# A strided row copy in HBM: half of the rows by way of SBUF, in two-batch transfers

## The chip, the core and the metric

The kernel runs on one core of a Trainium2 chip. Its time is device microseconds of one launch. No compute engine does any of the work: SyncE (SP) and ScalarE (ACT) only issue transfers, each on a hardware queue of its own, and the core's 16 DMA engines carry them out.

## What is computed

The reference takes every second row of the first 512 rows of each of 32 batches:

```python
batch, seq, dim = 32, 1024, 512
x = np.random.randn(batch, seq, dim).astype(np.float32)
start, stop, stride = 0, 512, 2
return x[:, start:stop:stride, :].astype(np.float32)
```

One row is 512 floats, 2 KB. The output has 32 x 256 = 8192 rows, 16.78 MB. In `x` a wanted row begins every 4 KB, and a batch every 2 MiB. In the output rows follow one another without a gap, and a batch begins every 512 KiB. Both tensors lie in HBM, so at least 16.78 MB are read there and 16.78 MB written.

## The kernel before

The file holds several ways to do this copy; the constant `STRATEGY` (line 10) picks `_d2d_2q` (line 43), and the other functions are never called. `_d2d_2q` issues one transfer for each batch, straight from `x` to the output within HBM, the even batches on SP and the odd ones on ACT (line 49). Each transfer is 256 rows, 512 KiB. Nothing is computed and no transfer depends on another.

Semaphores are put in by the tile framework. It uses eight in turn, four on each queue, so the fifth transfer of a queue is issued only after the first has landed. At the end SP waits for all of them (these waits carry line 241, where the framework's context closes).

Of the kernel before, what the change touches and what calls it, by code (L numbers as in the profile page):

```python
# [1 line left out]

# [4 lines left out]


STRATEGY = "d2d_2q"  # L10

SLAB_SHARES = (11, 11, 10)

D2D2_SHARES = (10, 10, 12)


def _d2d(tc, x, out, start, stop, stride):
    nc = tc.nc
    B = x.shape[0]
    src = x[:, start:stop:stride, :]  # L20
    engines = [nc.sync, nc.scalar, nc.gpsimd]
    chunks = [(b, min(b + 1, B)) for b in range(0, B, 1)]
    for i, (b0, b1) in enumerate(chunks):
        eng = engines[i % len(engines)]
        eng.dma_start(out[b0:b1], src[b0:b1])


def _d2d_slab(tc, x, out, start, stop, stride):
    nc = tc.nc
    B = x.shape[0]  # L30
    src = x[:, start:stop:stride, :]
    engines = [nc.sync, nc.scalar, nc.gpsimd]
    shares = SLAB_SHARES
    assert sum(shares) == B
    b0 = 0
    for eng, n in zip(engines, shares):
        if n <= 0:
            continue
        eng.dma_start(out[b0 : b0 + n], src[b0 : b0 + n])
        b0 += n  # L40


def _d2d_2q(tc, x, out, start, stop, stride):
    nc = tc.nc
    B = x.shape[0]
    src = x[:, start:stop:stride, :]
    engines = [nc.sync, nc.scalar]
    for b in range(B):
        engines[b % 2].dma_start(out[b : b + 1], src[b : b + 1])


def _d2d_2q_stagger(tc, x, out, start, stop, stride):
    nc = tc.nc
    B = x.shape[0]
    n_out = out.shape[1]
    half = n_out // 2
    src = x[:, start:stop:stride, :]

    def full(b):
        return (out[b : b + 1], src[b : b + 1])  # L60

    def halfc(b, h):
        r0 = h * half
        r1 = r0 + half
        return (out[b, r0:r1], src[b, r0:r1])

    sync_chunks = [full(b) for b in range(0, 30, 2)] + [halfc(30, 0), halfc(30, 1)]
    scalar_chunks = [halfc(1, 0)] + [full(b) for b in range(3, 32, 2)] + [halfc(1, 1)]
    assert len(sync_chunks) == len(scalar_chunks) == 17

    for (od, sd), (od2, sd2) in zip(sync_chunks, scalar_chunks):
        nc.sync.dma_start(od, sd)
        nc.scalar.dma_start(od2, sd2)


def _d2d_2q_faststart(tc, x, out, start, stop, stride):
    nc = tc.nc
    B = x.shape[0]
    n_out = out.shape[1]
    half = n_out // 2  # L80
    src = x[:, start:stop:stride, :]

    nc.gpsimd.dma_start(out[0, 0:half], src[0, 0:half])
    sync_chunks = [(out[0, half:n_out], src[0, half:n_out])] + [
        (out[b : b + 1], src[b : b + 1]) for b in range(2, 32, 2)
    ]
    scalar_chunks = [(out[b : b + 1], src[b : b + 1]) for b in range(1, 32, 2)]
    for i in range(max(len(sync_chunks), len(scalar_chunks))):
        if i < len(sync_chunks):
            nc.sync.dma_start(*sync_chunks[i])  # L90
        if i < len(scalar_chunks):
            nc.scalar.dma_start(*scalar_chunks[i])


def _d2d2(tc, x, out, start, stop, stride):
    nc = tc.nc
    B = x.shape[0]
    src = x[:, start:stop:stride, :]
    n_sync, n_scalar, n_pool = D2D2_SHARES
    assert n_sync + n_scalar + n_pool == B  # L100
    order = []
    order += [(nc.gpsimd, b) for b in range(n_sync + n_scalar, B)]
    for i in range(max(n_sync, n_scalar)):
        if i < n_sync:
            order.append((nc.sync, i))
        if i < n_scalar:
            order.append((nc.scalar, n_sync + i))
    for eng, b in order:
        eng.dma_start(out[b : b + 1], src[b : b + 1])


def _d2d3(tc, x, out, start, stop, stride, shares=(8, 8, 16)):
    nc = tc.nc
    B = x.shape[0]
    src = x[:, start:stop:stride, :]
    n_sync, n_scalar, n_pool = shares
    assert n_sync + n_scalar + n_pool == B
    seq = []
    iters = max(n_sync, n_scalar, max(1, n_pool // 2))
    bs = 0  # L120
    ba = n_sync
    bp = n_sync + n_scalar
    for i in range(iters):
        if i < n_sync:
            seq.append((nc.sync, bs + i))
        if i * 2 < n_pool:
            seq.append((nc.gpsimd, bp + 2 * i))
        if i < n_scalar:
            seq.append((nc.scalar, ba + i))
        if i * 2 + 1 < n_pool:  # L130
            seq.append((nc.gpsimd, bp + 2 * i + 1))
    assert len(seq) == B
    for eng, b in seq:
        eng.dma_start(out[b : b + 1], src[b : b + 1])


def _d2d_swdge(tc, x, out, start, stop, stride, nchunks=32):
    nc = tc.nc
    B = x.shape[0]
    src = x[:, start:stop:stride, :]  # L140
    step = B // nchunks
    for i in range(nchunks):
        b0 = i * step
        nc.gpsimd.dma_start(out[b0 : b0 + step], src[b0 : b0 + step])


def _d2d_hw2(tc, x, out, start, stop, stride, batches_per_chunk=2):
    nc = tc.nc
    B, S, D = x.shape
    n_out = out.shape[1]  # L150
    src = x[:, start:stop:stride, :]
    engines = [nc.sync, nc.scalar]
    bpc = batches_per_chunk
    chunks = [(b, min(b + bpc, B)) for b in range(0, B, bpc)]
    for i, (b0, b1) in enumerate(chunks):
        eng = engines[i % len(engines)]
        n = b1 - b0
        s_ap = src[b0:b1].transpose([1, 0, 2])
        d_ap = out[b0:b1].transpose([1, 0, 2])
        eng.dma_start(d_ap, s_ap)  # L160


def _sbuf_pipelined(ctx, tc, x, out, start, stop, stride):
    nc = tc.nc
    B, S, D = x.shape
    n_out = out.shape[1]
    q = 2
    P = 128
    assert n_out == q * P

    src = x[:, start:stop:stride, :]

    pool = ctx.enter_context(tc.tile_pool(name="io", bufs=6))
    for b in range(B):
        t = pool.tile([P, q * D], out.dtype, name="t")
        nc.sync.dma_start(t, src[b].rearrange("(p q) d -> p q d", q=q))
        nc.scalar.dma_start(out[b].rearrange("(p q) d -> p (q d)", q=q), t)


@with_exitstack  # L180
def kernel(
    ctx: ExitStack,
    tc: tile.TileContext,
    x: bass.AP,
    start: bass.AP,
    stop: bass.AP,
    stride: bass.AP,
    out: bass.AP,
):
    nc = tc.nc  # L190
    assert isinstance(start, int) and isinstance(stop, int) and isinstance(stride, int)

    if STRATEGY == "d2d":
        _d2d(tc, x, out, start, stop, stride)
    elif STRATEGY == "d2d_2q":
        _d2d_2q(tc, x, out, start, stop, stride)
    elif STRATEGY == "d2d_2q_stagger":
        _d2d_2q_stagger(tc, x, out, start, stop, stride)
    elif STRATEGY == "d2d_2q_faststart":
        _d2d_2q_faststart(tc, x, out, start, stop, stride)  # L200
    elif STRATEGY == "d2d_slab":
        _d2d_slab(tc, x, out, start, stop, stride)
    elif STRATEGY == "d2d2":
        _d2d2(tc, x, out, start, stop, stride)
    elif STRATEGY == "d2d3":
        _d2d3(tc, x, out, start, stop, stride)
    elif STRATEGY == "d2d_swdge":
        _d2d_swdge(tc, x, out, start, stop, stride)
    else:
        _sbuf_pipelined(ctx, tc, x, out, start, stop, stride)  # L210


# [1 line left out]
_INS = ['x', 'start', 'stop', 'stride']  # L214
_OUTS = [((32, 256, 512), 'float32')]
#: Inputs that are plain numbers.
_NUMBERS = {'start': 0, 'stop': 512, 'stride': 2}


# [26 lines left out]
```

## Time and profile before

| What | Value |
|---|---|
| time, median of 13 runs | 84.71 us (83.82 to 86.12) |
| the profiled execution's own time | 84.92 us |
| its span, first to last instruction | 83.1 us |
| transfers | 32 of 512 KiB |
| HBM traffic over the span | 404 GB/s, reads and writes together |

The span leaves out what a launch does around the first and last instruction; in the profiled execution that is 84.92 - 83.1 = 1.8 us. In the profile q1 and q10 are the two hardware queues. A packet is here one row of 2 KB, or a small one that raises a semaphore. The share of a queue is the time that its packets took, added up, as a share of 16 engines' span. GB/s counts each copied byte once, though a copy within HBM touches HBM twice. Instructions that issue transfers are not counted as busy, so a table of engines is nearly empty for this kernel.

### The profile page before, as it was taken

Reading aid. Unit: us, or ns where it says so; the run is one execution under the profiler, and the core shown is the slowest. Engines: PE = TensorE matmul, PEld = TensorE weight load, DVE = VectorE, ACT = ScalarE, POOL = GpSimd, SP = SyncE. Lnnn points to the kernel's source line nnn. Section 1 sums busy time; section 2 is a strip of 40 time slices with the busy share of each in tenths; the row PEclk is TensorE's granted clock in tenths of the full one; section 3 lists DMA queues with packets and bytes.
Section 4 is the critical chain, followed back from the end, with each engine's and each line's share of the span. In section 5 each row is a group of like instructions: output and inputs, shape, how many; then the busy total and the mean of one; then the engine's idle time right before and its main releaser. Section 6 shows DMA issues by size and latency. Waiting matters only on the chain. (4 is left out here: it accounts for less than half of the span.)

```text
span 83.1 us, 77 instructions
## 1 busy us (share of the span) xinstructions
POOL 0.2 (0%) x4
## 2 busy tenths in 40 slices
POOL 0000000000000000000000000000000000000000
DMA  0989998999999799999989989997888999998950
GB/s 0 215 217 133 270 214 171 260 198 208 197 227 228 189 200 255 220 211 222 192 203 232 209 154 251 234 225 211 172 272 198 194 229 235 215 241 200 195 164 14
DMA packets 8704, 16.78 MB, mean 202 GB/s; under 512 B 512, under 2 KB 512, under 8 KB 8704
## 3 DMA queue, kind: packets, MB, share of 16 engines
q1 hardware_dynamic: 4352, 8.39, 49.9%
q10 hardware_dynamic: 4352, 8.39, 39.2%
HBM read 16.78 MB, written 16.78 MB: 404 GB/s over the span
## 5 line engine op out<-in xcount | busy, mean ns | idle before, releaser
L227 POOL MEMSET const-bfloat16-1.0<- 128x1 bf16 x1 | 0.1, 101 | 0.0
L227 POOL MEMSET const-uint8-127<- 128x1 uint8 x1 | 0.1, 101 | 0.0
L227 POOL MEMSET const-float32-0.0<- 128x1 f32 x1 | 0.1, 98 | 0.2 <-issue 0.2
L227 POOL MEMSET const-float32-1.0<- 128x1 f32 x1 | 0.1, 98 | 0.0
## 6 DMA issues: line engine op xcount, KB each, us to landing
out_dram<-in_x_dram ACTq DMA_DIRECT2D x16, 512.0 KB, 19.3
out_dram<-in_x_dram SPq DMA_DIRECT2D x16, 512.0 KB, 19.5
```

What stands on the lines that cost most here:

```text
L227: nc = _bacc.Bacc("TRN2", target_bir_lowering=False, num_devices=1)
```

## The change

The new kernel splits the rows of each batch by the parity of their number in the output. One parity is copied directly within HBM, as before; the other is loaded into SBUF and stored from there. Which parity goes which way alternates with bit 1 of the batch number (`apart`).

Each transfer covers one parity of two batches, ordered row by row: row 0 of the first batch, row 0 of the second, row 2 of the first, and so on (`two`). That is again 256 rows of 2 KB.

The batches are treated in four groups of eight. The pairs differ by kind of transfer. Loads take neighbours (0 and 1, 2 and 3, ...). Direct copies take 0 and 5, 2 and 7, 1 and 4, 3 and 6. Stores take batches four apart (0 and 4, 1 and 5, ...).

SP issues all 16 loads, ACT all 16 direct copies. Then, group by group, both wait until the four loads of the group have landed, and the group's four stores are issued in turn on SP and ACT. One SBUF tile (`held`, 128 partitions x 32 x 512 floats) keeps the whole staged half, so no buffer is reused. Semaphores are placed by hand: one for each group's loads, and one for each queue's remaining transfers, on which SP waits at the end.

```diff
-STRATEGY = "d2d_2q"
+EIGHT = 8
+def apart(b):
+    return 1 - (b >> 1 & 1)
+def two(t, b, step, parity):
+    return t[b : b + step + 1 : step].rearrange("b (p two) d -> two p b d", two=2)[parity]
...
-def _d2d_2q(tc, x, out, start, stop, stride):
-    nc = tc.nc
-    B = x.shape[0]
-    src = x[:, start:stop:stride, :]
-    engines = [nc.sync, nc.scalar]
-    for b in range(B):
-        engines[b % 2].dma_start(out[b : b + 1], src[b : b + 1])
...
     src = x[:, start:stop:stride, :]
+    B, rows, D = out.shape
+    P = rows // 2
+    sp, act = nc.sync, nc.scalar
+    groups = range(0, B, EIGHT)
+    with tc.tile_pool(name="io", bufs=1) as io:
+        held = io.tile([P, B, D], x.dtype, name="held")
+        with tc.tile_critical():
+            loaded = [nc.alloc_semaphore(name=f"loaded{g}") for g in groups]
+            done = [nc.alloc_semaphore(name=f"done{i}") for i in range(2)]
+            for g in groups:
+                for i, (b, step) in enumerate(((0, 5), (2, 5), (1, 3), (3, 3))):
+                    b += g
+                    at = g + 2 * i
+                    sp.dma_start(held[:, at : at + 2], two(src, at, 1, 1 - apart(at))).then_inc(loaded[g // EIGHT], 16)
+                    act.dma_start(two(out, b, step, apart(b)), two(src, b, step, apart(b))).then_inc(done[1], 16)
+            for g in groups:
+                for queue in (sp, act):
+                    queue.wait_ge(loaded[g // EIGHT], 16 * 4)
+                for b in range(g, g + 4):
+                    k = b % 2
+                    to = two(out, b, 4, 1 - apart(b))
+                    (sp, act)[k].dma_start(to, held[:, b : b + 5 : 4]).then_inc(done[k], 16)
+            sp.wait_ge(done[0], 16 * (B // 4))
+            sp.wait_ge(done[1], 16 * (B // 2 + B // 4))
```

More of the change, by code (lines that the diff above doesn't have):

```diff
@@ L2 @@
-from contextlib import ExitStack
 import concourse.bass as bass
 import concourse.tile as tile
-from concourse import bass_utils, mybir
-from concourse._compat import with_exitstack
-STRATEGY = "d2d_2q"
-SLAB_SHARES = (11, 11, 10)
-D2D2_SHARES = (10, 10, 12)
-def _d2d(tc, x, out, start, stop, stride):
+from concourse import mybir
+EIGHT = 8
[3 more added lines that the diff above has]
+    return t[b : b + step + 1 : step].rearrange("b (p two) d -> two p b d", two=2)[parity]
@@ L18, in _d2d, with kernel @@
+def kernel(tc, x, start, stop, stride, out):
     nc = tc.nc
-    B = x.shape[0]
     src = x[:, start:stop:stride, :]
[L21 to L28, printed above, removed]
-    nc = tc.nc
-    B = x.shape[0]
-    src = x[:, start:stop:stride, :]
[L32 to L40, printed above, removed]
@@ L43, in _d2d_2q @@
-def _d2d_2q(tc, x, out, start, stop, stride):
-    nc = tc.nc
-    B = x.shape[0]
-    src = x[:, start:stop:stride, :]
-    engines = [nc.sync, nc.scalar]
-    for b in range(B):
[L49 to L73, printed above, removed]
@@ L76, in _d2d_2q_faststart @@
[L76 to L92, printed above, removed]
@@ L95, in _d2d2 @@
[L95 to L109, printed above, removed]
@@ L112, in _d2d3 @@
[L112 to L134, printed above, removed]
@@ L137, in _d2d_swdge @@
[L137 to L160, printed above, removed]
@@ L163, in _sbuf_pipelined @@
[L163 to L177, printed above, removed]
@@ L180 @@
[L180 to L210, printed above, removed]
+    B, rows, D = out.shape
```

## The prediction

> **What bounds the kernel now.** I read the page's head first, then the DMA rows, then the waits of SP's own queue, then the stretches of time. The head and the rows of the page:
>
> ```profile
> span 83.1 us, 77 instructions
> ...
> GB/s 0 215 217 133 270 214 171 260 198 208 197 227 228 189 200 255 220 211 222 192 203 232 209 154 251 234 225 211 172 272 198 194 229 235 215 241 200 195 164 14
> DMA packets 8704, 16.78 MB, mean 202 GB/s; under 512 B 512, under 2 KB 512, under 8 KB 8704
> ...
> q1 hardware_dynamic: 4352, 8.39, 49.9%
> q10 hardware_dynamic: 4352, 8.39, 39.2%
> HBM read 16.78 MB, written 16.78 MB: 404 GB/s over the span
> ...
> out_dram<-in_x_dram ACTq DMA_DIRECT2D x16, 512.0 KB, 19.3
> out_dram<-in_x_dram SPq DMA_DIRECT2D x16, 512.0 KB, 19.5
> ```
>
> No compute engine works; everything is 8192 packets of one 2 KB row each, plus 512 small ones that count semaphores. The two queues together hold the 16 DMA engines for 49.9 + 39.2 = 89.1% of the span, 74.0 us of 83.1. Divided among the rows that is 0.891 x 83.1 x 16 / 8192 = 145 ns for one row. The second row of numbers is rates in slices of 2.1 us: they swing from 133 to 272 about a mean near 214.
>
> ```profile
> SPq L49 <- DMA out_dram<-in_x_dram: 50.9, 12, 5.0
> ```
>
> SP's queue waits 50.9 us in all before it issues, but that starves nobody: a transfer lands 19.4 us after its issue, and eight transfers of 524,288 bytes at 214 GB/s take 19.6 us, so eight stand queued at all times. The stretches show the same:
>
> ```profile
> 0.00:2.00 2.00, 0.20 (x4) 1.00 0.00 0
> ...
> 40.00:48.00 8.00, 0.00 (x0) 1.00 0.97 215
> 48.00:56.00 8.00, 0.00 (x0) 1.00 0.98 215
> ...
> 78.00:80.00 2.00, 0.00 (x0) 1.00 0.93 214
> 80.00:81.00 1.00, 0.00 (x0) 1.00 0.29 96
> ```
>
> The last two columns are the engines' busy share and GB/s. From 2 to 80 us the engines are held 95% of the time at about 214 GB/s. So the kernel is 78.0 us of steady copying, and 84.9 - 78.0 = 6.9 us of everything else (2 us before the first packet, 3 us of thinning out and closing, 1.8 us outside the span). The profiled execution took 84.92 us, 0.2 over the median of 84.71.
>
> **Why a row takes 145 ns** decides the case. The packet records of the trace, sorted by duration, have a minimum of 81 ns and a median of 84 ns; 83% are under 150 ns, and the rest, up to 1.5 us long, hold half of all packet time. A row passes at 84 ns when nothing is in its way; 16 engines at that pace would copy 2048 x 16 / 84 = 390 GB/s, which asks 780 GB/s of HBM (each byte read there and written there). What they get is 214, or 428 GB/s of HBM. So the rows stall on something about HBM, in bursts.
>
> **The change, part by part.**
>
> *The direct half.* 16 transfers instead of 32, all on ACT, each 256 rows of 2 KB again: 4096 rows remain, each read and written in HBM.
>
> *The staged half, added.* 16 loads on SP (4096 rows into one SBUF tile) and later 16 stores, eight on each queue (4096 rows again). The engines now pass 12,288 rows instead of 8192: half as many again. HBM still carries 16.78 MB each way. At 84 ns a row the added work is 4096 x 84 / 16 = 21.5 us of every engine. The profile shows no row to or from SBUF, so this is bounded: the floor is the fastest direct row (81 ns), as such a row would do all of a load's reading as well; the ceiling is the present 145 ns, stalls and all. I take 84 ns, since only one end of a staged row lies in HBM and the stall seems to come from there.
>
> *First stage: loads beside direct copies.* Both queues have 16 transfers of 256 rows. I assume that they advance alike: here q1 and q10 copied 8.39 MB each and ended within about one transfer of each other. The stage is 8192 rows, 25.2 MB of HBM traffic (8.39 x 3). The floor is no stall: 8192 x 84 / 16 = 43.0 us, at the present 95% occupation 45.3 us. It asks 556 GB/s of HBM, which the best slices of before nearly reach (272 x 2 = 544, or 46.3 us for the stage). The ceiling is the present mean of 428 GB/s: 25.2 / 428 = 58.8 us. The choice is between 46.3 and 58.8. I take a point a fifth of the way up, 48.8 us (516 GB/s), because free-running demand falls from 780 GB/s to 585, and bursts of queueing should shrink by more than the demand does.
>
> *Second stage: stores alone.* 4096 rows, written to HBM only. Floor 21.5 / 0.95 = 22.6 us (371 GB/s); ceiling the present write rate of 214 GB/s, 39.2 us. I take 22.6: a store at 84 ns asks for 390 GB/s of HBM, less than the 428 it gives now.
>
> *Issues and waits.* 48 transfers instead of 32. An issue takes 0.51 us in the trace (up to 2.1 us among the first), so 24 on each engine are some 13 to 20 us, under 71 us of transfers: no cost while the queues stay full. Without that cover it would be 0.5 us apiece. SP waits for each group's loads before its stores, and behind that wait stand only the later stores; ACT's waits stand likewise behind its 16 direct copies. By then the first group's four loads are long landed, and the last group is waited for with the other three groups' stores queued. Cost 0; if loads lagged the direct copies, ACT's stores would be late by the lag, one transfer's time, about 2 us. The semaphores that were reused after eight transfers go, with the 50.9 us of waits, worth nothing as shown. Start and close are as before, bounded by 0 and 1 us for the hand-made section; I take 0.
>
> *Pairs of batches.* A load reads two batches 2 MiB apart alternately; a store writes two batches that lie 4 x 512 KiB = 2 MiB apart; the direct copies use distances of 3 or 5 batches. In the trace SP and ACT work on neighbouring batches, 2 MiB apart in x, and the mean of 214 GB/s already includes what that does. The Trainium skill speaks against such steps: the page "DMA: Bandwidth & Descriptors", section "Latency and other measured facts", gives copies at a row pitch of 512 KiB 207 GB/s and at 2 MiB 164, a factor of 1.26. Applied to the loads' half of the first stage and to the second stage it adds 0.26 x (24.4 + 22.6) = 12.2 us, and the sum would be 90 us. Here the pitch between the rows of different partitions is 8 KiB at the source and 4 KiB at the output, only two batches alternate, and the row of before stands nearer: I take no cost, and leave it in the range.
>
> *Sum.* 48.8 + 22.6 + 6.9 = 78.3 us against the execution's 84.9; against the median 78.1. That is 7.8% less.
>
> A second rule weighs on the first stage. The page "HBM Reference", section "Specifications (TRN2)", states some 425 GB/s for one core alone, bounded by its DMA engines, and 716 for the stack. The trace's 428 GB/s is that figure, but as reads plus writes, with only 214 GB/s through the engines. If 425 is what a core gets from HBM in any mix, both stages together take at least 33.55 / 425 = 78.9 us and nothing is gained; if it is the engines' limit, the floors above stand, since 12,288 rows at 425 GB/s are 59.2 us. The 272 of single slices (544 in HBM) speaks against a hard 425.
>
> **Rivals.**
>
> 1. *The staged half runs free.* Stalls vanish in both stages: 45.3 + 22.6 + 6.9 = 74.8 us, and at the page's 425 GB/s for every row down to 59.2 + 6.9 = 66.1. For it: the median row of 84 ns. Against: the first stage still asks more of HBM than the mean of now.
>
> 2. *HBM traffic is the limit, whatever the path* (the other side). The first stage then holds at 428 GB/s, 58.8 us, and the stores, now bound by the engines at 371 GB/s, leave HBM capacity unused: 58.8 + 22.6 + 6.9 = 88.3 us. For it: the evenness of the stretches (208 to 225 GB/s over 8 us) and the 425 of the page. Against: slices of 272. It decides above 55.4 us for the first stage (78.0 - 22.6), that is below 455 GB/s; in rows, a mean over all 12,288 of more than about 96 ns (74.0 x 16 / 12,288).
>
> 3. *Writes are the limit.* HBM takes 214 GB/s of writes: the stores alone need 39.2 us, the first stage 45.3: 91.4 us. For it: nothing in the trace separates reads from writes. Against: only the same swing of rates.
>
> 4. *The change gives what it takes*, stage one near 455 GB/s: 84.7.
>
> **How the numbers follow.** Relief in part, 76 to 82 us: 0.42, with 78.1 as its time and 76 to 82 its own range. Rival 1, below 76: 0.28, a third of it under 72.5. A small gain between 82 and 84.3: 0.04. Within 0.5% (about what the measurement can tell): 0.03. Rivals 2 and 3 and the pitch rule, 85.2 to 91.4: 0.23, half of it above 87.5. So faster 0.74, same 0.03, slower 0.23. The range of 72.5 to 87.5 leaves out about 0.1 at each end.
>
> **What would show it.** The packets become about 13,000 and 25.2 MB; the rate in the slices rises to about 340 GB/s for the first 49 us (516 in HBM, of which two thirds pass as rows) and to some 370 for the last 23. Stores at 214 GB/s would prove rival 3 right; a first stage of 285 GB/s, rival 2. If there is a hole between the stages, the waits cost what I put at nothing. If one queue runs out much earlier, the assumption of alike advance is wrong. The prediction fails if the mean row stays above 96 ns.

## The result, and the profile after

The changed kernel takes 80.84 us (median of 11 runs, 80.63 to 82.12) against 84.44 us for the kernel before (median of 48). The ratio is 0.961, with a 95% interval of 0.958 to 0.964: 3.6 us less. The ratio leaves out slow runs, those more than 1.5% above the fastest of the same kernel, so it is not the quotient of the two medians. The forecast was 78.1 us, with a range of 72.5 to 87.5 and 76 to 82 for the likeliest case. The direction and the range hold. The reason does not, and most of this part is about that.

The page of the changed kernel (its profiled execution took 81.09 us), with the rows that answer to those shown of before:

```profile
span 79.3 us, 99 instructions
...
GB/s 0 247 331 270 264 260 331 357 341 240 388 366 393 372 352 340 231 305 358 348 356 344 315 366 347 290 289 412 406 405 374 348 346 348 354 352 357 355 228 5
DMA packets 13057, 25.17 MB, mean 317 GB/s; under 512 B 769, under 2 KB 769, under 8 KB 13057
...
q1 hardware_dynamic: 6528, 12.58, 48.6%
q10 hardware_dynamic: 6528, 12.58, 47.5%
...
HBM read 16.78 MB, written 16.78 MB: 423 GB/s over the span
```

The engines carry half as many bytes again (25.17 MB), HBM the same as before. The two queues hold the engines for 48.6 + 47.5 = 96.1% of the span. That is 76.2 us, more than the 74.0 us of before, in a span that is 3.8 us shorter: packets now follow one another with hardly a gap between the first, at 2.0 us, and the last, at 77.7 us.

The two stages, in the view by stretches of time (length, POOL's busy time, TensorE's clock, share of the DMA engines, GB/s), and the one wait of SP's queue for loads:

```profile
2.00:54.50 52.50, 0.00 (x0) 1.00 1.01 325
54.50:77.00 22.50, 0.00 (x0) 1.00 1.04 359
```

```profile
SPq L47 <- DMA held<-in_x_dram: 0.5, 1, 0.5
```

A share above 1 means that packet records of one engine overlap in time. Counted in packet records, the first 8192 rows end at 53.9 us, so the first stage took 51.9 us and the second 23.8 (predicted 48.8 and 22.6). The wait for the loads cost nothing: 0.5 us, with direct copies still queued on ACT.

### The profile page after: what moved, and what is told of

Same layout as the page of the kernel before. It is cut to its first block, busy times and chain, and to the rows that moved or that the text cites. A ratio compares the mean times of both kernels' runs of the same rounds, so it can differ in the third digit from the quotient of the medians.

```text
span 79.3 us, 99 instructions
## 1 busy us (share of the span) xinstructions
POOL 0.2 (0%) x4
## 2 busy tenths in 40 slices
DMA packets 13057, 25.17 MB, mean 317 GB/s; under 512 B 769, under 2 KB 769, under 8 KB 13057
## 3 DMA queue, kind: packets, MB, share of 16 engines
q1 hardware_dynamic: 6528, 12.58, 48.6%
q10 hardware_dynamic: 6528, 12.58, 47.5%
```

## The experiments

The theory on record says that rows stall on HBM demand of the moment, and that staging half of the rows lowers it. Its rivals: a fixed ceiling of HBM traffic, a ceiling of writes, the order of rows and the pairs of batches. In each group of runs below the kernel before ran on the same chip; its medians there lie between 83.3 and 83.9 us. Where no ratio is given, the run is one profiled execution.

### One part alone: all rows direct, in the new transfers

```diff
-sp.dma_start(held[:, at : at + 2], two(src, at, 1, 1 - apart(at))).then_inc(loaded[g // EIGHT], 16)
-act.dma_start(two(out, b, step, apart(b)), two(src, b, step, apart(b))).then_inc(done[1], 16)
+for k, parity in enumerate((apart(b), 1 - apart(b))):
+    (sp, act)[k].dma_start(two(out, b, step, parity), two(src, b, step, parity)).then_inc(done[k], 16)
...
-(the stores and their waits)
```

> All 8192 rows go directly, in the change's two-batch transfers and pairs, no staging. If the gain comes from the SBUF route, this stays at the time of before, 84 to 85 us (8192 rows at about 145 ns). If it comes from the order of rows and the pairs of batches, it falls to 81 us or most of the way.

Measured: 84.49 us, ratio 1.014 (1.007 to 1.021). The new transfers and pairs by themselves bring nothing and may cost a little.

### The same transfers in turn

```diff
-for g in groups:            # SP: loads, ACT: direct copies, side by side
+for g in groups:            # loads on both queues; then stores on both; then:
...
+for g in groups:
+    for i, (b, step) in enumerate(((0, 5), (2, 5), (1, 3), (3, 3))):
+        b += g
+        (sp, act)[i % 2].dma_start(two(out, b, step, apart(b)), two(src, b, step, apart(b))).then_inc(done[i % 2], 16)
```

> The same 48 transfers as the change, but the direct copies come last, alone, each kind on both queues. If working side by side is what saves: loads 22.6 + stores 22.6 + direct copies at 214 GB/s 39.2 + 5.2 around = 89.6 us. If it makes no difference beside what a row of each kind costs anyway: 81 us. If HBM traffic is the limit whatever the path, loads and stores at their engine-bound pace leave it unused, and the time is again near 90.

Measured: 83.53 us, ratio 1.007 (1.002 to 1.012). That is 2.65 us slower than its companion with loads and direct copies side by side (neighbouring pairs, below, 80.88 us), but 6 us faster than I had worked out, and the stretches show why. Loads run from 2 to 29 us, stores to about 55, direct copies to 80:

```profile
2.00:8.00 6.00, 0.00 (x0) 1.00 0.95 286
8.00:16.00 8.00, 0.00 (x0) 1.00 0.99 301
16.00:24.00 8.00, 0.00 (x0) 1.00 1.03 371
24.00:29.00 5.00, 0.00 (x0) 1.00 1.00 317
29.00:46.00 17.00, 0.00 (x0) 1.00 1.05 367
46.00:55.00 9.00, 0.00 (x0) 1.00 1.09 240
55.00:80.00 25.00, 0.00 (x0) 1.00 0.97 324
```

Direct copies alone run at 324 GB/s, not at the 214 of the kernel before. That is 648 GB/s of HBM traffic for 25 us, so there is no ceiling near 428, nor one of 214 for writes: rivals 2 and 3 fall. The loads are slower than expected instead.

Counted in packet records (neighbouring stages overlap a little at the borders), the first 4096 rows (loads) took 26.3 us rather than 22.6, the next (stores) 25.8 and the last (direct copies) 26.1. Loads and direct copies make 52.4 us, hardly more than the 51.9 of the changed kernel's first stage: side by side saves little. The larger part of the loss is in the stores, 25.8 us against 23.8, and the stretches show it where the stores end and the direct copies begin, 9 us at 240 GB/s.

### Neighbours in every pair

```diff
-for i, (b, step) in enumerate(((0, 5), (2, 5), (1, 3), (3, 3))):
+for i in range(4):          # loads, direct copies and stores all take batches at, at + 1
```

> The change with neighbouring batches in every pair, direct copies and stores too. If a power-of-two distance of the two batches of a store costs, stores 512 KiB apart instead of 2 MiB get no slower and the time is 81 us or below; if the choice of pairs carries the gain, it goes back toward 84 us. My theory puts the pairs at nothing: 80.5 to 81.5.

Measured: 80.88 us, ratio 0.971 (0.967 to 0.976). The changed kernel did not run in this group, so its ratio to before can't be set against this one closely; in microseconds the two differ by 0.04. The choice of pairs carries at most a small part of the gain.

### Direct copies beside loads and beside stores

```diff
+for i in range(0, 16, 4):
+    copy(0), load(1, i)
+    load(0, i + 1), copy(1)
+    load(0, i + 2), load(1, i + 3)
...
+    copy(0), store(1, g)
+    store(0, g + 1), copy(1)
+    store(0, g + 2), store(1, g + 3)
```

> Eight of the direct copies beside the loads, eight beside the stores, never two at once. If HBM's mixed traffic has a ceiling near the 477 GB/s of the changed kernel's first stage, an even demand of 520 at free pace runs at that ceiling: 33.55 / 477 = 70.3 us + 5.2 around = 75.5 us. If each direct row carries its own stall of some 38 ns (first stage: (103 - 84) x 2), the mean row is 84 + 38 / 3 = 97 ns and the time stays at 79.5 to 81. If writes beside direct copies stall more than reads do, above 81.

Measured: 84.12 us, ratio 1.012 (1.005 to 1.020). That is 3.2 us above the run of neighbouring pairs in the same group. Evening out the demand makes the kernel slower, against both of my theories of stalls; only the third expectation, writes beside direct copies, foresaw it. The stretch with the stores is the slower one, though stores by themselves are quicker than loads (23.8 us in the changed kernel, against 26.3 in turn):

```profile
2.00:43.00 41.00, 0.00 (x0) 1.00 0.99 327
43.00:80.00 37.00, 0.00 (x0) 1.00 1.01 318
```

By packet records the two halves of the work, 6144 rows each, took 39.1 and 39.3 us. Eight direct copies cost about 13.1 us (half of the 26.1 in turn). The half with the loads is therefore a plain sum: 26.3 + 13.1 = 39.4. The half with the stores is not: 23.8 + 13.1 = 36.9, so 2.4 us are lost where direct copies run beside stores. The run in turn lost 2.0 us where they meet. The changed kernel keeps the two nearly apart. Why they disturb each other stays open.

### Why were the direct copies fast? Half of them alone, all in two passes, all twice

In turn, the direct copies had run over memory that loads and stores had visited, and in another order than before. Three runs take this apart. The first copies only the half that the change copies directly (no loads, no stores). The second goes on with the other half, copied directly too. The third copies everything twice in the manner of before.

```diff
+for other in range(2):      # half alone: without this loop, with other = 0
+    for g in groups:
+        for i, (b, step) in enumerate(((0, 5), (2, 5), (1, 3), (3, 3))):
+            b += g
+            parity = apart(b) ^ other
+            (sp, act)[i % 2].dma_start(two(out, b, step, parity), two(src, b, step, parity)).then_inc(done[i % 2], 16)
```

> Only the 16 direct copies, as they ran last and alone in the experiment in turn, where they took about 25 us (335 GB/s); loads and stores are left out, so half of the output stays unwritten. If the order of the copies (two batches, one parity, the two queues on different pairs) makes a direct row fast: again 25 us, a span of about 30. If they were fast because the loads and stores had been over the same memory shortly before: 214 GB/s, 39 us, a span of about 44.

Measured: 33.5 us, a span of 31.7; packets run from 2.4 to 30.2 us, 27.9 us for half of the rows, without any earlier visit.

> All rows direct, first one parity of all batches, then the other, each pass with the order of the copies of the experiment before. If the order makes them fast: two passes of 25 us, about 56 us in all. If only memory that was gone over before is fast: 39 + 25 = 64, about 70 us. If neither, two passes of 39 us: 84 us.

Measured: 81.62 us, ratio 0.984 (0.974 to 0.995). None of the three expectations: the first pass is fast and the second slow. The two stretches lie within the passes:

```profile
4.00:29.00 25.00, 0.00 (x0) 1.00 0.99 319
33.00:77.00 44.00, 0.00 (x0) 1.00 0.88 166
```

> The copy of before done twice in one launch, the second pass after the first has landed. If the first visit to a stretch of memory is what stalls a row, the second pass takes about 50 us (335 GB/s) after a first of 80. If a stall belongs to reading and writing HBM at once, both passes take 80 us.

Measured: 163.65 us; the stretch of the first pass has 218 GB/s, that of the second 216. An earlier visit changes nothing:

```profile
2.00:78.00 76.00, 0.00 (x0) 1.00 0.95 218
84.00:158.00 74.00, 0.00 (x0) 1.00 0.96 216
```

So the same kind of transfer, by the same code, copies one half of the rows at nearly twice the rate of the other (319 and 166 GB/s). **The new theory**: it is the rows themselves. The function `apart` sorts them into two classes, by whether the parity of the output row differs from bit 1 of the batch number. A row of the first class is copied within HBM quickly, one of the second slowly. The change copies the quick class directly and sends the slow class by way of SBUF.

### The classes exchanged, and the other class alone

```diff
-    return 1 - (b >> 1 & 1)
+    return b >> 1 & 1
```

> The change with the two parities exchanged: what was copied directly is staged, what was staged is copied directly; nothing else differs. New theory: the rows of one class (parity of the row differs from bit 1 of the batch) pass quickly as direct copies, those of the other class slowly (27 and 48 us for half of the rows, two passes). Then the first stage grows by about 21 us, from 53 to 74, and the time is 96 to 102 us. Old theory (staging relieves stalls, whatever the row): no difference, 80 to 81.5.

Measured: 107.0 us, ratio 1.277 (1.266 to 1.288). It is one exchanged bit, with the same number, size, order and queues of transfers. The stretches put the whole loss in the first stage:

```profile
2.00:80.00 78.00, 0.00 (x0) 1.00 0.94 218
80.00:103.00 23.00, 0.00 (x0) 1.00 1.01 353
```

The stores, now of the quick class, are as before: 353 GB/s against 359. The time is above the 96 to 102 us expected: the first stage ran 77.5 us instead of 51.9, 25.6 more, where 21 had been worked out. The slow class alone, in the next run, takes 51.4 us; with 26.3 for the loads that makes 77.7.

> The 16 direct copies of the other class alone, from a fresh start; half of the output is not written. If the class of the row decides: about 48 us of copying, a span of 52, at 165 to 175 GB/s from the beginning. If the second pass of the experiment in two passes was slow because it came second: 27 us, a span of 32.

Measured: 57.08 us, a span of 55.3; packets run from 2.4 to 53.8 us. The slow class is slow from the start and all the way, so the second pass was not slow because it came second. A stretch within the copying of each class alone, first the quick one, then the slow one:

```profile
4.00:28.00 24.00, 0.00 (x0) 1.00 0.98 307
```

```profile
4.00:52.00 48.00, 0.00 (x0) 1.00 0.89 162
```

27.9 us for the one half and 51.4 for the other make 79.3 us. The kernel before needs 79.8 from its first packet to its last: its 214 GB/s is, nearly, the mean of two kinds of row. Only nearly, since each run alone has a start and an end of its own: class after class in one launch, the two passes took 26.4 and 48.9 us, 75.3 in all. Rows of both classes beside each other seem to cost something more, and no run says why.

### The distance of the loads' batches

```diff
-sp.dma_start(held[:, at : at + 2], two(src, at, 1, 1 - apart(at))).then_inc(loaded[g // EIGHT], 16)
+at, far = ((1, 3), (3, 3), (0, 5), (2, 5))[i]
+at += g
+sp.dma_start(held[:, at : at + far + 1 : far], two(src, at, far, 1 - apart(at))).then_inc(loaded[g // EIGHT], 16)
```

> The change, with loads that pair batches 3 and 5 apart (as the direct copies do, a step behind them) instead of neighbours 2 MiB apart. If the power-of-two distance is what holds the loads at 305 GB/s in the experiment in turn (27.5 us where 22.6 were expected), the first stage shortens by up to 5 us: 76 to 79. If not, 80.5 to 81.5.

> The changed kernel itself, on the chip of these runs, as the mark for the two beside it: 80.8 us, 0.961 of before.

Measured side by side: 80.47 us, ratio 0.961 (0.954 to 0.968), and 80.37 us, ratio 0.960 (0.952 to 0.969). The 2 MiB between the two batches of a load cost nothing.

### One parity for all batches

```diff
-    return 1 - (b >> 1 & 1)
+    return 1
```

> The change with the odd rows of every batch copied directly and the even rows of every batch staged, so bit 1 of the batch number no longer plays a part. If the class of a row is its parity together with that bit, half of the direct copies are now of the slow class: midway between 80.4 and 107.0, about 93.7 us, and the direct copies of batches 0, 5, 1, 4 of each group land quickly, those of 2, 7, 3, 6 slowly. If the parity alone decides: 80.4 or 107.

Measured: 90.65 us, ratio 1.092 (1.083 to 1.100). The first stage ends with its 8192nd row at 66.0 us, 64.0 us after its first. The changed kernel's stage ran 51.9 us and that of the exchanged classes 77.5 us; midway is 64.7. The landings of the direct copies, in order (a landing is the time at which the trace has 16 more increments of the queue's semaphore), alternate as expected up to the last, the second being the first slow one:

```
us from one direct copy's landing to the next
one parity   5.5 3.8 4.7 3.2 4.3 3.7 4.2 3.9 4.5 3.5 4.5 3.5 4.4 3.5 3.0
the change   5.5 2.7 2.9 3.9 2.5 2.8 2.7 3.1 4.1 3.1 2.7 3.3 2.9 3.6 2.8
exchanged    5.0 5.6 5.0 4.4 5.5 4.5 5.2 4.6 5.1 4.8 4.3 5.1 5.3 4.5 3.9
```

So bit 1 of the batch number belongs to the rule. Most of the 3 us by which the run undercuts 93.7 comes from a place that I had not thought of, the stores:

```profile
2.00:64.00 62.00, 0.00 (x0) 1.00 0.95 259
66.00:86.00 20.00, 0.00 (x0) 1.00 1.05 408
```

All stores of even rows run at 408 GB/s, in 21.0 us, and nearly every packet takes 84 ns; the alternating stores of the change run at 359, in 23.8 us.

## Why the prediction was right, and where it was not

**Why a row takes 145 ns: wrong, and it is the step that failed.** The prediction saw two kinds of packet, 83% quick and the rest stalled, and put the stalls down to HBM demand of the moment. They depend on which row is copied directly. By packet records the mean is 102 ns in the quick class alone and 176 ns in the slow one (median 84 in both; 69% of the slow class's records are under 150 ns too, and which rows of it stall is not shown). The profile of before could hardly tell this, since each transfer holds rows of both classes. Nor do packet records tell it where two queues run beside each other: with the classes exchanged, the loads' records average 149 ns and those of the slow direct copies 133. But the name and the bit in `apart` were in the diff, and the prediction passed over what they choose.

**The number came near by luck.** The argument would have been the same for any half of the rows. With rows of both classes copied directly (one parity), the first stage ran 64.0 us, above the 58.8 that the prediction took for the ceiling, and the kernel was 9% slower than before. With the slow class it ran 77.5. Lower demand brought no relief in either.

**The first stage: 48.8 us predicted, 51.9 measured.** At 22.6 us for the loads, the 48.8 leave 26.2 for the direct half. In turn the quick class took 26.1 us and the loads 26.3. So the term of the sum that is too low is the 84 ns for a load, "since only one end of a staged row lies in HBM": by packet records a load took 102 ns in the run in turn. Its rate there is 286 GB/s in the first 6 us, 301 up to 16 us, 371 up to 24 and 317 up to 29. The quick class alone, without loads, starts slowly too (262 GB/s in the first 6 us, 298 up to 16 us, 324 up to 28), and no run says why.

**The second stage: 22.6 predicted, 23.8 measured.** The 84 ns were right for stores of one parity (21.0 us) and too low for those of the change, which took 94 ns by packet records.

**What the staged half is worth.** A staged half costs 26.3 us of loads and 23.8 of stores, 50.1 in all; the slow class copied directly costs 51.4 alone and 48.9 as a second pass. Staging is therefore hardly cheaper than the slow direct copy. Two direct passes without any staging took 81.62 us, ratio 0.984; the change, on the same chip, 80.37 us, ratio 0.960. All rows direct with the classes beside each other, on another chip, had 1.014. So a good part of the gain seems to come from keeping the classes apart in time, the rest from the SBUF route; the intervals are too wide to divide it exactly.

**Side by side.** Alike advance held: the last load landed at 53.9 us and the last direct copy at 55.7.

**Issues, waits, start and close: right.** There is no hole between the stages, and the waits for loads took 0.5 us. From the last packet to the end of the span pass 1.6 us, against 1.2 before.

**Pairs of batches: right at nothing.** The rule on power-of-two pitches (the Trainium skill, "DMA: Bandwidth & Descriptors", "Latency and other measured facts") would have put the sum at 90 us by the prediction's estimate. Moving the loads off 2 MiB gave 80.47 against 80.37 us.

**The 425 GB/s of a core** (the Trainium skill, "HBM Reference", "Specifications (TRN2)"). Read as a limit of HBM traffic in any mix, it is refuted by the quick class alone, 2 x 307 = 614 GB/s.

**The test that I set myself was off.** "The prediction fails if the mean row stays above 96 ns": it is 0.961 x 79.3 x 16 / 12,288 = 99 ns, and the kernel is faster. The threshold took 95% occupation as given; the occupation rose to about 101%, which offsets it.

**The rivals.** Rivals 1, 2 and 3 are out: the first stage ran neither free nor at 428 GB/s, and stores were not held to 214. Rival 4 needed 455 GB/s in the first stage, and it had 25.2 / 51.9 = 485.

## What to carry to other kernels

When half of the packets' time lies in a slow tail, ask which rows are slow before asking what slows them: run one half of the data alone, then the other. Here a copy within HBM ran at 307 GB/s for one half of the rows and at 162 for the other, at equal size and stride, and the average over both looked like a limit of the hardware. If a diff sorts the work by a bit of an address or an index, exchange that bit first: it was one line, and it moved the time by 26.6 us. And try direct copies beside loads rather than beside stores: here the one was a plain sum, the other lost 2.4 us.

## What was not expected of the hardware

- Direct copies of 2 KB rows within HBM ran at 307 GB/s for one class of rows and 162 for the other. The class is given by bit 0 of the output row and bit 1 of the batch, that is by steps of 2 KB and 1 MiB in the output, of 4 KB and 4 MiB in `x`. Neither end of a slow row is slow by itself: the same rows were loaded in 26.3 us and stored in 23.8, and stores of the quick class were no faster (24.0). The 51.4 us of the direct copy are close to the sum of the two. That its two addresses meet in the same part of HBM would fit, but is only argued: no run moved a row to another destination.
- Stores of one parity from SBUF ran at 408 GB/s; stores whose parity changed every two transfers at 359. A version of the change whose stores take one parity of all groups and then the other was not tried.
- Quick direct copies beside loads took what each takes in turn (39.1 us against 39.4 in sum); beside stores they took 39.3 us against 36.9. The reason is open.
